# GpSimd takes the sums of h for both parts, and three weight loads are placed anew, in a two-layer trunk on one NeuronCore

## The chip, the cores and the metric

The kernel runs on one core of one Trainium2 chip, as one launch. The metric is the time of the whole launch in microseconds (us). Before the change, three runs gave 2854.96, 2854.89 and 2853.45 us; their median, 2854.89, is the time before. The profile comes from another execution, which took 2849.49 us. In the profile PE is the engine of the matmuls (PEld its weight loads), DVE the vector engine, ACT the scalar engine, POOL GpSimd, and SP the engine that issues the DMAs.

## The reference

One inference step of a trunk with two layers on 1024 frames of a new stream and 32 frames of a running one (1056 columns), width 1024. Layer 0 mixes with retention (4 heads), layer 1 with gated linear attention, GLA (4 heads); after each comes a convolutional feed-forward network of inner width 2816. Cut to what matters:

```
def conv_ffn(h, conv_state, w_up, conv_w, conv_b, w_down):
    u = h @ w_up
    ext = concatenate([conv_state, u], axis=1)
    c = conv_b + sum over j of ext[:, j:j + T] * conv_w[j]      # 3 taps
    gate, val = split(c, 2, axis=-1)
    return (silu(gate) * val) @ w_down, ext[:, T:]

def trunk(x, ...):
    for i in range(2):
        h = rmsnorm(x, norm_mix[i])
        y, S = retention_mixer(h, ...) if i == 0 else gla_mixer(h, ...)
        x = x + y
        h = rmsnorm(x, norm_ffn[i])
        y, cs = conv_ffn(h, ...)
        x = x + y
    return rmsnorm(x, norm_final), states and caches
```

## The kernel before

Every float32 operand of a matmul is split into a high and a low part, and a product takes three matmuls: high by high, high by low, low by high. ACT casts the high part (`whi`, `wgh`, `XA`), DVE subtracts it from the source for the low part (`wlo`, `wgl`). The large products work on pairs of weight tiles and pairs of column blocks with seven products in place of eight (`seven`, matmuls at L333, L337, L338; 264 columns each, 12 matmuls a product). For that, sums and differences of weights (`pair_weights`, L297 on, DVE at L310 to L316) and of activations are formed. `snap` copies a product from PSUM by ACT (L569, L1471, L1536); `put` adds one into its place by DVE (L1532).

The order of the instructions on every engine is made ahead: the program is written once, as a list of instructions with their dependencies, and a list scheduler with a cost model of its own then sets each engine's queue. `order(a, b)` puts a behind b. SP issues nearly all DMAs in its own order, and a DMA waits there for its buffer.

The stages, in us of the profile:

- 0 to 66, the opening: x comes in three column chunks `xc`, the first in four parts, and the first products of `w_rg` run (L124 to L126). `load_w` loads one 512 KB weight tile and splits it. Squares of x go to `NB` for the norm.
- 66 to 358, the pairs: gate, query and key projections, 14 pairs f. `operands(1)` prepares the second half of the columns in `NB` with eight scalings by ACT (L538) and sums by DVE (L543, L547), ahead of `load(0)`, the first pair's weights. The cosines and sines are multiplied by the norm R on DVE (L606).
- 358 to 905, retention and its output product.
- 909 to 1363, the up product of layer 0: `ffn_up` takes 22 f of 14 products, about 20.3 us each; after the last product of an f, `conv` convolves it and writes h to DRAM, `scr_h` (22 rows of tiles).
- 1363 to 1625, the down product: class `Pieces` takes h in two parts p of 8 tiles in the seven-product form, and the other 6 tiles follow plainly. Part one reads sums of h that are formed during the up product (`load_h`, `sum_h`, `sums_out`: four sums k of two tiles, DVE L1386, through `scr_s`); its operands come as 14 loads of 528 KB through a queue (`pull`, L1396). Part two loads 1.08 MB whole for each of four column blocks (`staged`, L1418) and forms its sums on DVE (`minus`, L1432, four for each s), just ahead of the casts (L1427).
- 1630 to 1960, GLA: four heads in three column chunks; the next head's weights `w_gqk` are loaded and split where they are first used (L104), the score tile A is masked (L1000, `copy_predicated`) and multiplied.
- 1960 to 2847, layer 1's output product, up product (2132 to 2590), down product and the last norm, with the same code.

Of the kernel before, what the change touches and what calls it, by code (L numbers as in the profile page):

```python
# [52 lines left out]
def trunk_kernel(ctx: ExitStack, tc: tile.TileContext, io):  # L53
# [45 lines left out]
    def load_w(src, dst=None, after=None):  # L99
        i = uid()  # L100
        raw = raw_tile(f"raw{i}")
        nc.sync.dma_start(raw, src)
        hi, lo = dst or (w_tile(f"whi{i}"), w_tile(f"wlo{i}"))
        ins = S.copy(hi, raw), V.tensor_tensor(lo, raw, hi.bitcast(F32), op=ALU.subtract)  # L104
        if after is not None:
            for a, b in zip(ins, after):
                order(a, b)
        return hi, lo

    ahead = {}  # L110
# [20 lines left out]
    sqb = [2]  # L131

    def sumsq(ss, kt, src, n, on_dve=False):
        def square(dst):
            if on_dve:
                V.tensor_tensor(dst, src, src, op=ALU.mult)
            else:
                S.activation(dst, src, AF.Square)
# [158 lines left out]
    def pair_weights(sa, sb):  # L297
# [5 lines left out]
        def split(src, name):  # L303
            h, l_ = w_tile(f"{name}h{uid()}"), w_tile(f"{name}l{uid()}")
            S.copy(h, src)  # L305
            V.tensor_tensor(l_, src, h.bitcast(F32), op=ALU.subtract)  # L306
# [3 lines left out]
        V.tensor_tensor(rv[:, a], rv[:, a], rv[:, b], op=ALU.add)  # L310
        V.tensor_tensor(rg[:, a], rv[:, a], rg[:, a], op=ALU.subtract)
        V.tensor_tensor(rg[:, b], rg[:, b], rg[:, a], op=ALU.subtract)
# [3 lines left out]
        V.tensor_tensor(rv[:, b], rv[:, b], rg[:, a], op=ALU.subtract)  # L316
# [89 lines left out]
    def opening(cs, SA, RE, NB, gn):  # L406
# [17 lines left out]
        xs, w01 = [], []  # L424
        sqb[0] = 4
        nps[0] = Arena(NB, ss=(384, 4), sq=(384, 4), dg=(384, 1), tm=(6, 2))
        with pool("x0", bufs=3, side="right") as xp:
            for c, (c0, n) in enumerate(CM):
                xc = xp.tile([P, KT, 384], F32, tag="xc", name=f"xc{c0}")
                step = 2 if c == 0 else 8  # L430
                for kt in range(0, KT, step):
                    nc.sync.dma_start(xc[:, kt:kt + step, :n], io["xT"][:, kt:kt + step, c0:c0 + n])
                    if c == 0 and kt in (0, 6):
                        w01.append(load_w(io["w_rg"][kt // 6]))
# [3 lines left out]
            nc.sync.dma_start(sin, io["sin"])  # L438
            nc.sync.dma_start(SA, io["xT"][:, :, 0:2 * TH])
# [67 lines left out]
    def pairs_phase(cs, SA, sp, UR, NB, gn, xp, finish, then):  # L507
# [19 lines left out]
        steps = []  # L527

        def operands(s):
# [7 lines left out]
            def scale(kt):  # L537
                return lambda: S.activation(st[:, kt], st[:, kt], AF.Copy, scale=gcol[:, 0, kt:kt + 1])  # L538
# [18 lines left out]
        X[1].update(zip((7, 4), rooms_of(sp.tile([P, 2 * sz], F32R, tag="SA", name="SA1"), 2)))  # L557
        operands(1)
        later(steps, 8)
# [7 lines left out]
        def snap(b):  # L567
            t = up.tile([P, TH], F32, tag="sn", name=f"sn{uid()}", bufs=6)
            S.copy(t, b)  # L569
# [1357 lines left out]
```

## Time and profile before

| what | value |
|---|---|
| median of three runs | 2854.89 us |
| the profiled execution's own time | 2849.49 us |
| its span | 2847.7 us |
| TensorE: first matmul starts at | 9.12 us |
| TensorE busy | 2784.6 us |
| DVE, ACT, POOL busy | 2109.5, 1320.2, 278.5 us |
| bytes moved by DMA | 419.35 MB, mean 147 GB/s |

The page's rows give an engine's busy time with its share of the span, and how many instructions it ran. A row of a timeline gives the start, the duration, the engine, the kernel's line, the operation and its tiles (out<-in), and in brackets how long the engine had stood idle ahead of it and what it waited for. In rows by line, "x24" is a count, and where three numbers stand behind it, they are the least, the median and the largest duration in ns.

### The profile page before, as it was taken

What the parts mean: (1) busy time and instruction counts of PE and PEld (TensorE: products, weight loads), DVE (VectorE), ACT (ScalarE), POOL (GpSimd) and SP (SyncE); (2) the same over time, 40 slices, a digit from 0 to 9 for tenths busy, and PEclk for the clock granted to TensorE, in tenths of its full rate; (3) what the DMA queues carried; (4) which work ended last, traced back from release to release, by engine and by line L of the source; (5) the groups of instructions that cost most, each with busy time, mean ns of one, the idle gap of its engine ahead of it and who ended that gap; (6) DMA issues with size and microseconds to landing.
All of it is one profiled execution on the core that took longest, in us unless ns stands there. A gap on an engine that the chain in (4) does not pass through costs nothing.

```text
span 2847.7 us, 52541 instructions
## 1 busy us (share of the span) xinstructions
PE 2784.6 (98%) x20954; PEld 2681.9 (94%) x20954; DVE 2109.5 (74%) x3506; ACT 1320.2 (46%) x2395; POOL 278.5 (10%) x516
## 2 busy tenths in 40 slices
PE   8999999999999999999999999999999999999998
PEld 7999977888999999999999899999999999999997
DVE  7777777777578877877775677774478878788756
ACT  8433344444455444445443555553245444445424
POOL 1000000000001111111000232220011111110001
PEclk9999999999999999999999999999999999999999
DMA  6333386664865223332866301114522233428673
GB/s 218 110 123 106 118 269 205 213 198 150 273 203 192 76 75 121 129 129 94 284 216 240 122 27 46 52 44 143 198 85 75 73 116 115 150 70 278 205 232 116
DMA packets 232326, 419.35 MB, mean 147 GB/s; under 512 B 27376, under 2 KB 145776, under 8 KB 231056
## 3 DMA queue, kind: packets, MB, share of 16 engines
q1 hardware_dynamic: 231536, 415.40, 43.6%
q8 instruction: 164, 2.69, 0.4%
q14 instruction: 82, 0.67, 0.1%
q10 hardware_dynamic: 544, 0.59, 0.1%
HBM read 292.08 MB, written 123.85 MB: 146 GB/s over the span
## 4 chain that ended last, share of the span: by engine, by line
PE 82%; DVE 7%; DMA 4%; ACT 4%; issue 1%; POOL 1%; SPq 0%; DVEq 0%; ACTq 0%; POOLq 0%
PE pu L338 16%; PE pu L333 16%; PE pu L337 16%; PE pd L1281 4%; PE pd L1280 4%; PE pd L1282 4%; PE psv L238 2%; PE psv L237 1%; PE psv L236 1%; PE pj L124 1%; PE pj L126 1%; PE pj L125 1%; PE pg L124 1%; PE pg L125 1%; PE pg L126 1%
## 5 line engine op out<-in xcount | busy, mean ns | idle before, releaser
L104 DVE TENSOR_TENSOR wlo<-raw,whi 128x1024 fp32r<-128x1024 f32 x146 | 180.7, 1241 | 100.9 <-ACT whi L104 44.9
L1536 ACT COPY AR<-pu 128x264 f32<-128x264 f32 x264 | 99.0, 375 | 295.2 <-PE pu L338 292.4
L338 PE MATMUL pu<-XA,wgl 128*128 128x264 f32 x752 | 213.6, 284 | 0.0
L333 PE MATMUL pu<-XA,wgh 128*128 128x264 f32 x752 | 213.0, 283 | 0.0
L337 PE MATMUL pu<-XA,wgh 128*128 128x264 f32 x752 | 213.0, 283 | 0.0
L104 ACT CAST whi<-raw 128x1024 fp32r<-128x1024 f32 x146 | 152.3, 1048 | 110.7 <-DMA raw<-w_ro 38.0
L1280 PE MATMUL pd<-XB,whi 128*128 128x264 f32 x552 | 157.9, 286 | 1.6 <-DVE rm L208 1.6
L1558 DVE SCALAR_TENSOR_TENSOR AR<-AR,cw 128x1058 f32<-128x1058 f32 x88 | 115.8, 1317 | 57.7 <-ACT AR L1557 57.4
L1282 PE MATMUL pd<-XB,wlo 128*128 128x264 f32 x552 | 157.0, 284 | 0.0
L1281 PE MATMUL pd<-XB,whi 128*128 128x264 f32 x552 | 156.7, 284 | 0.0
L333 PE MATMUL pu<-XA,wsh 128*128 128x264 f32 x520 | 148.6, 286 | 1.7 <-ACT AR L1536 0.9
L338 PE MATMUL pu<-XA,wsl 128*128 128x264 f32 x520 | 148.3, 285 | 0.8 <-DVE wsl L306 0.8
L337 PE MATMUL pu<-XA,wsh 128*128 128x264 f32 x520 | 147.7, 284 | 0.0
L1532 DVE TENSOR_TENSOR AR<-AR,pu 128x264 f32<-128x264 f32 (+2 forms) x440 | 144.6, 368 | 0.0
L306 DVE TENSOR_TENSOR wtl<-rv,wth 128x1024 fp32r<-128x1024 f32 x58 | 71.6, 1234 | 98.5 <-ACT wth L305 97.1
L333 PEld LDWEIGHTS pu<-XA,wgh 128*128 128x128 f32 x752 | 141.3, 188 | 0.0
L338 PEld LDWEIGHTS pu<-XA,wgl 128*128 128x128 f32 x752 | 141.2, 188 | 0.0
L337 PEld LDWEIGHTS pu<-XA,wgh 128*128 128x128 f32 x752 | 141.2, 188 | 0.0
L333 PE MATMUL pu<-XA,whi 128*128 128x264 f32 x448 | 127.5, 285 | 1.8 <-ACT XA L1427 1.2
L338 PE MATMUL pu<-XA,wlo 128*128 128x264 f32 x448 | 127.1, 285 | 1.6 <-DVE wlo L104 1.6
L337 PE MATMUL pu<-XA,whi 128*128 128x264 f32 x448 | 126.9, 284 | 0.5 <-DVE XA L1412 0.3
L333 PE MATMUL pu<-XA,wth 128*128 128x264 f32 x408 | 116.4, 285 | 0.7 <-ACT wth L305 0.7
(481 smaller groups left out, 10528.0 us busy)
## 6 DMA issues: line engine op xcount, KB each, us to landing
raw<-w_ro SPq DMA_DIRECT2D x52, 512.0 KB, 4.7
rg<-w_up SPq DMA_DIRECT2D x44, 512.0 KB, 3.6
rv<-w_up SPq DMA_DIRECT2D x44, 512.0 KB, 3.5
scr_h<-AR SPq DMA_DIRECT2D x44, 512.0 KB, 2.7
AR<-scr_x SPq DMA_DIRECT2D x32, 528.0 KB, 4.9
scr_x<-AR SPq DMA_DIRECT2D x32, 528.0 KB, 3.5
raw<-scr_w SPq DMA_DIRECT2D x32, 512.0 KB, 4.8
AR<-scr_h SPq DMA_DIRECT2D x28, 528.0 KB, 4.8
```

The source lines that it names most:

```text
L104: ins = S.copy(hi, raw), V.tensor_tensor(lo, raw, hi.bitcast(F32), op=ALU.subtract)
L124: PE.matmul(ps, hi[:, k], rh, start=kt == 0, stop=False)
L306: V.tensor_tensor(l_, src, h.bitcast(F32), op=ALU.subtract)
L333: mm = PE.matmul(ps, wh[:, k], x[:, 0, kt], start=m in (1, 2, 4, 5) and kt == 0, stop=False, skip_group_check=True)
L337: PE.matmul(ps, wh[:, k], x[:, 1, kt], start=False, stop=False, skip_group_check=True)
L338: mm = PE.matmul(ps, wl[:, k], x[:, 0, kt], start=False, stop=kt == 3, skip_group_check=True)
L1280: PE.matmul(o, w[0][:, k], h[0][:, :n], start=i == 0, stop=False)
L1281: PE.matmul(o, w[0][:, k], h[1][:, :n], start=False, stop=False)
L1282: self.last_mm = PE.matmul(o, w[1][:, k], h[0][:, :n], start=False, stop=i == nk - 1)
L1532: V.tensor_tensor(u[:, d:d + n], t[:, o:o + n], b[:, o:o + n], op=op)
L1536: S.copy(t, b)
L1558: V.scalar_tensor_tensor(cj, uj[:, 1:T + 3], cw[:, nt, 1:2], cj, op0=ALU.mult, op1=ALU.add)
```

## The change

Five parts.

1. Opening. `load_w` may load, cast and subtract in halves; the first weight tile does so, with a part of x between. The small load `rgn` goes behind `sin`. The squares of the first chunk come behind the cast of the second weight tile.
2. Start of the pairs. `load(0)` is written ahead of `operands(1)`, whose scalings come behind the last cast of the weights or the last snapshot; cosine and sine are multiplied by GpSimd. `pair_weights` takes the engine of its sums: GpSimd for f = 1 and 2 of the pairs and f = 1 of each up product.
3. Sums of h for both parts: eight of four instructions each in a layer (before: four), on GpSimd, at the products `SUMS`; `scr_s` grows from 4 to 8.
4. Part two of the down product reads its operands through the same queue as part one (28 loads of 528 KB through four slots); `staged` and the sixteen subtractions are gone.
5. GLA. The next head's `w_gqk` are loaded in chunk 1 of a head, and the low parts are ordered behind that chunk's last mask.

```diff
-    def load_w(src, dst=None, after=None):
+    def load_w(src, dst=None, parts=1, between=None):
...
+        for j in range(parts):
+            k = slice(j * D // parts, (j + 1) * D // parts)
+            nc.sync.dma_start(raw[:, k], src[:, k])
+            last_w[:] = S.copy(hi[:, k], raw[:, k]), V.tensor_tensor(lo[:, k], raw[:, k], hi[:, k].bitcast(F32),
+                                                                     op=ALU.subtract)
+            if between and j + 1 < parts:
+                between()
...
-    def pair_weights(sa, sb):
+    def pair_weights(sa, sb, E=V):
...
-        V.tensor_tensor(rv[:, a], rv[:, a], rv[:, b], op=ALU.add)
+        E.tensor_tensor(rv[:, a], rv[:, a], rv[:, b], op=ALU.add)
...
+                if c == 0:
+                    part(0, 2)
+                    w01.append(load_w(io["w_rg"][0], parts=2, between=lambda: part(2, 2)))
+                    part(4, 2)
+                    part(6, 2)
+                    w01.append(load_w(io["w_rg"][1]))
+                    first_w[:] = last_w
+                else:
+                    part(0, KT)
...
             nc.sync.dma_start(sin, io["sin"])
+            nc.sync.dma_start(gn, io["rgn"])
...
-                    sumsq(stage[c], kt, xs[c][:, kt, :CM[c][1]], CM[c][1])
+                    sumsq(stage[c], kt, xs[c][:, kt, :CM[c][1]], CM[c][1], first_w[0] if c == 0 else None)
...
+                    ins = S.activation(st[:, kt], st[:, kt], AF.Copy, scale=gcol[:, 0, kt:kt + 1])
+                    if s:
+                        order(ins, snaps[-1] if snaps else last_w[0])
...
-            W[f] = pair_weights(*src)
+            W[f] = pair_weights(*src, G if f in (1, 2) else V)
...
         load(0)
+        X[1].update(zip((7, 4), rooms_of(sp.tile([P, 2 * sz], F32R, tag="SA", name="SA1"), 2)))
+        operands(1)
+        later(steps, 2)
...
-                V.tensor_tensor(t, t, R, op=ALU.mult)
+                G.tensor_tensor(t, t, R, op=ALU.mult)
...
-            later(steps, 1)
+            later(steps, 3 if n in (0, 2) else 1)
...
+            h, c = u
+            if c == 1 and h + 1 < GH:
+                for j in range(2):
+                    preload(("w_gqk", h + 1, j))
+                    order(last_w[1], mask[0])
...
+    SUMS = (42, 56, 70, 84, 97, 109, 121, 133)
...
-                order(nc.sync.dma_start(self.v[:, a], scr_h[k + 4 * a].rearrange("p (q t) -> p q t", q=4)), after)
+                order(nc.sync.dma_start(self.v[:, a], scr_h[k + k // 4 * 4 + 4 * a].rearrange("p (q t) -> p q t", q=4)),
+                      after)
...
-            V.tensor_tensor(d, a, b, op=ALU.subtract)
+            G.tensor_tensor(d, a, b, op=ALU.subtract)
...
-    def part_one(self):
-            for s in range(2):
+    def operands(self):
+            for p, s in ((0, 0), (0, 1), (1, 0), (1, 1)):
...
-            self.todo += [split(1, b11), minus(b12, b12, b11), split(2, b21), split(5, b12), minus(b12, b22, b12),
-                          split(6, b12), minus(b11, b12, b11), split(7, b11), minus(b21, b12, b21), split(4, b21),
-                          split(3, b22)]
...
-                        if s:
-                            for j in range(2):
-                                self.staged(1, s, j)
-                        self.operands(s)
+                        self.splits()
...
-                    self.step()
+                    self.step(1 if p or q else 2)
...
-            W[f] = pair_weights(io["w_up"][l, f], io["w_up"][l, NF + f])
+            W[f] = pair_weights(io["w_up"][l, f], io["w_up"][l, NF + f], G if f == 1 else V)
...
-            if s == 1 and i % 2 == 0 and 8 <= f <= 16 and f % 2:
-                nxt.sum_h(i // 2)
-            if s == 0 and i == 5 and 8 <= f <= 16:
-                if f % 2 == 0:
-                    if f > 8:
-                        nxt.sums_out((f - 10) // 2)
-                    if f < 16:
-                        nxt.load_h((f - 8) // 2, stored[0])
+            for j, at in enumerate(SUMS if s == 0 else ()):
+                if k == at + 12:
+                    nxt.sums_out(j)
+                if k == at:
+                    nxt.load_h(j, stored[0])
+                if k - at in (5, 7, 9, 11):
+                    nxt.sum_h((k - at - 5) // 2)
```

Three places show what the scheduler makes of it. The first is ACT's queue at the start of the pairs, from the first pair's first cast (`wg`) to the first snapshot (`sn`, the copy of the first product); RE is the gate that the opening leaves, NB the second half of the columns, being scaled. Before:

```order
L305 CAST wgh_649<-rg_645 128x1024
L379 ACTIVATE RE_84<-RE_84 128x768
L383 ACTIVATE RE_84<-RE_84,rgn 128x384 x2
L538 ACTIVATE NB_628<-NB_628,gcol 128x528 x8
L379 ACTIVATE RE_84<-RE_84 128x576
L314 CAST wv_656<-rv_646 128x512
L383 ACTIVATE RE_84<-RE_84,rgn 128x288 x2
L305 CAST wsh_660<-rg_645 128x1024
L569 COPY sn_681<-pu_668 128x264
```

And with the change:

```order
L309 CAST wgh_641<-rg_637 128x1024
L382 ACTIVATE RE_83<-RE_83 128x768
L317 CAST wv_648<-rv_638 128x512
L386 ACTIVATE RE_83<-RE_83,rgn 128x384 x2
L309 CAST wsh_652<-rg_637 128x1024
L309 CAST wth_656<-rv_638 128x1024
L382 ACTIVATE RE_83<-RE_83 128x576
L551 ACTIVATE NB_661<-NB_661,gcol 128x528
L386 ACTIVATE RE_83<-RE_83,rgn 128x288 x2
L551 ACTIVATE NB_661<-NB_661,gcol 128x528
L582 COPY sn_678<-pu_665 128x264
L551 ACTIVATE NB_661<-NB_661,gcol 128x528 x4
```

Six of the eight scalings now stand behind the first snapshot (one and one ahead of it, four right behind), and the cast of `wt` has come ahead of it.

The second is SP's queue in the down product, around the first weight loads of the part's last pairs; L1480, L1489 and their successors L1482, L1491 bring the residual and store a result. Before, with the two whole loads of part two's first half (L1418):

```order
L1480 DMA AR_7512<-scr_x 128x2x528
L102 DMA raw_15949<-w_dn 128x1024
L1489 DMA scr_x<-AR_7512 256x1x528
L1480 DMA AR_7512<-scr_x 128x2x528
L102 DMA raw_15955<-scr_w 128x1024
L102 DMA raw_15961<-scr_w 128x1024
L1418 DMA AR_7512<-scr_h 128x8x264
L1489 DMA scr_x<-AR_7512 256x1x528
L1418 DMA AR_7512<-scr_h 128x8x264
L1444 DMA rv_15968<-w_dn 128x512
```

With the change, where the pieces come by L1420 (the first of the three from `scr_h` ends part one, the next two begin part two):

```order
L1491 DMA scr_x<-AR_7515 256x1x528
L1482 DMA AR_7515<-scr_x 128x2x528
L1420 DMA AR_7515<-scr_h 128x4x264 x3
L1420 DMA AR_7515<-scr_s 128x4x264
L1491 DMA scr_x<-AR_7515 256x1x528
L1482 DMA AR_7515<-scr_x 128x2x528
L1420 DMA AR_7515<-scr_s 128x4x264 x2
L105 DMA raw_15983<-w_dn 128x1024
L1491 DMA scr_x<-AR_7515 256x1x528
L105 DMA raw_15989<-scr_w 128x1024
L105 DMA raw_15995<-scr_w 128x1024
```

The five pieces that open part two now stand ahead of the weight load that the two whole loads stood behind.

The third is the place of the sums of h in the up product: before on DVE, between the puts (L1532), convolutions (L1558, L1562) and weight splits (L306):

```order
L1562 TENSOR_TENSOR AR_7512<-AR_7512 128x1058
L310 TENSOR_TENSOR rv_11959<-rv_11959 128x512
L306 TENSOR_TENSOR wtl_11746<-rv_11727,wth_11745 128x1024
L1532 TENSOR_TENSOR AR_7512<-AR_7512,pu_11886 128x232
L1532 TENSOR_TENSOR AR_7512<-AR_7512,pu_11886 128x32
L1532 TENSOR_TENSOR AR_7512<-AR_7512,pu_11931 128x264
L1532 TENSOR_TENSOR AR_7512<-AR_7512,pu_11831 128x264
L1386 TENSOR_TENSOR AR_7512<-AR_7512 128x2x264 x2
L1558 SCALAR_TENSOR_TENSOR AR_7512<-AR_7512,cw_7506 128x1058
L306 TENSOR_TENSOR wgl_11963<-rg_11958,wgh_11962 128x1024
```

and with the change on POOL, where all four stand together between the copies of one convolution into the cache (L1549, L1550):

```order
L1541 COPY AR_7515<-cc_7510 128x2
L1549 COPY cst_7511<-AR_7515 128x2
L1550 COPY cst_7511<-AR_7515 128x2
L1410 TENSOR_TENSOR AR_7515<-AR_7515 128x2x264 x4
L1549 COPY cst_7511<-AR_7515 128x2
L1550 COPY cst_7511<-AR_7515 128x2
L1541 COPY AR_7515<-cc_7510 128x2
```

The four sums of a group have left DVE's queue and follow one another on POOL with nothing between them.

More of the change, by code (lines that the diff above doesn't have):

```diff
@@ L97, in w_tile @@
         return wp.tile([P, D], F32R, tag="w", name=name, bufs=10)
-    def load_w(src, dst=None, after=None):
+    def load_w(src, dst=None, parts=1, between=None):
         i = uid()
         raw = raw_tile(f"raw{i}")
-        nc.sync.dma_start(raw, src)
         hi, lo = dst or (w_tile(f"whi{i}"), w_tile(f"wlo{i}"))
[L104 to L107, printed above, removed]
+        for j in range(parts):
[5 more added lines that the diff above has]
+                between()
         return hi, lo
+    last_w = []
     ahead = {}
@@ L131, in trunk_kernel, with sumsq @@
     sqb = [2]
-    def sumsq(ss, kt, src, n, on_dve=False):
+    last_sq = [None]
+    def sumsq(ss, kt, src, n, after=None):
         def square(dst):
[L135 to L138, printed above, removed]
+            ins = S.activation(dst, src, AF.Square)
+            if after is not None:
+                order(ins, after)
+            last_sq[0] = ins
         s_ = ss[kt % len(ss)]
@@ L1025, in gla @@
         state = {}
+        mask = [None]
         def mix(h, c, u):
```

58 lines of the change are left out of this document (16 added, 42 removed).

## Prediction

> **What bounds the kernel now.** I read the busy shares first, then the chain that ended last, then windows cut along the stages. In the window rows, "TensorE busy" is the second number, the share near the end is the granted clock, and the difference between window length and PE busy is time TensorE stood still.
>
> ```profile
> PE 2784.6 (98%) x20954; PEld 2681.9 (94%) x20954; DVE 2109.5 (74%) x3506; ACT 1320.2 (46%) x2395; POOL 278.5 (10%) x516
> PE 82%; DVE 7%; DMA 4%; ACT 4%; issue 1%; POOL 1%; SPq 0%; DVEq 0%; ACTq 0%; POOLq 0%
> core 0: us, PE busy (x) PEld busy (x) DVE busy (x) ACT busy (x) POOL busy (x), PEclk, DMA share, GB/s
> 0.00:66.00 66.00, 55.62 (x332) 54.03 (x333) 49.26 (x76) 53.18 (x96) 12.06 (x17) 1.00 0.68 234
> 66.00:77.00 11.00, 7.45 (x48) 7.03 (x47) 10.47 (x12) 10.94 (x17) 0.00 (x0) 0.84 0.24 86
> 905.00:940.00 35.00, 32.44 (x255) 31.31 (x255) 32.04 (x52) 17.05 (x29) 2.49 (x5) 1.00 0.26 77
> 940.00:1340.00 400.00, 400.00 (x3299) 400.00 (x3298) 320.82 (x471) 183.12 (x258) 55.53 (x139) 1.00 0.30 104
> 1092.40:1112.70 20.30, 20.30 (x170) 20.30 (x169) 16.88 (x26) 9.13 (x14) 3.13 (x7) 1.00 0.38 132
> 1340.00:1385.00 45.00, 42.17 (x335) 40.76 (x334) 41.39 (x49) 32.40 (x40) 3.37 (x8) 1.00 0.81 259
> 1450.00:1470.00 20.00, 17.81 (x126) 16.84 (x125) 14.09 (x17) 7.52 (x10) 0.00 (x0) 0.91 0.75 257
> 1630.00:1960.00 330.00, 322.96 (x2701) 305.54 (x2699) 244.33 (x595) 179.82 (x578) 87.61 (x125) 0.99 0.14 45
> 2675.00:2695.00 20.00, 17.29 (x133) 16.25 (x132) 14.55 (x17) 8.09 (x12) 0.00 (x0) 1.00 0.81 273
> ```
>
> TensorE is busy for 98% of the span, and the change removes none of its matmuls. So all that can be won lies in TensorE's holes and in the slow clock behind them. The rows size the holes: 10.4 us in 0 to 66, 3.55 us in 66 to 77, 2.6 at the start of the up product, none at all between 940 and 1340, 2.8 around the change to the down product, 2.2 and 2.7 in the two 20 us windows at the down product's second part, 7.0 over GLA's 330 us. Work taken from another engine inside 940 to 1340 gains nothing, however large it is; there the only question is whether a hole appears.
>
> **The change part by part.** *Opening.*
>
> ```profile
> 1.19 0.42 SPq L67 DMA_DIRECT2D rgn<-rgn  x1
> 1.66 4.44 DMA xc<-xT
> 6.19 1.12 ACT L153 ACTIVATE XA<-xc,gcol 128x384 fp32r<-128x384 f32 x2 [4.18 <-DMA xc<-xT]
> 7.22 0.92 ACT L138 ACTIVATE NB<-xc 128x384 f32<-128x384 f32 x2
> 8.04 1.03 ACT L104 CAST whi<-raw 128x1024 fp32r<-128x1024 f32 x1
> 9.12 0.69 PE L124 MATMUL pj<-XA,whi 128*128 128x384 f32 x1 [9.12 <-ACT whi L104]
> 17.27 0.44 PE L126 MATMUL pj<-XA,wlo 128*128 128x384 f32 x1 [0.59 <-DVE wlo L104]
> ```
>
> SP issues the small rgn load at 1.19 and the first x at 1.66; with rgn moved behind sin, x goes 0.47 us earlier and ACT's split of x ends near 6.84 instead of 7.31. Behind it stood two squares (0.92 us) and a whole cast (1.03 us). Now the squares wait for a later cast, and the cast of half a weight comes next, about 0.52 us: TensorE starts near 7.4 in place of 9.12, which is 1.7 us, and the stop of 0.59 us at 17.27 goes, since the low half is also ready in halves. That is 2.3 us at most; I count 1.9, because x's later parts still come at the loads' pace and one more transfer is now interleaved.
>
> *Start of the pairs.*
>
> ```profile
> 55.55 1.25 DVE L606 TENSOR_TENSOR cos<-cos,R 128x1056 f32<-128x1056 f32 x1
> 62.94 5.13 ACT L538 ACTIVATE NB<-NB,gcol 128x528 f32<-128x528 f32 x8 [0.35 <-DMA NB<-xT]
> 69.92 1.04 ACT L305 CAST wsh<-rg 128x1024 fp32r<-128x1024 f32 x1
> 71.28 0.39 PE L333 MATMUL pu<-XS,wsh 128*128 128x264 f32 x1 [2.41 <-ACT sn L569]
> 72.93 0.59 PE L338 MATMUL pu<-XS,wsl 128*128 128x264 f32 x1 [1.14 <-DVE wsl L306]
> ```
>
> The two stops, 2.41 and 1.14 us, make up the whole 3.55 us of the window, and its clock of 0.84 over 11 us costs another 0.16 x 11 = 1.8 us: 5.3 in all. Both come from ACT and DVE being full (10.94 and 10.47 of 11). ACT's eight scalings (5.13 us) now stand mostly behind the first snapshot: six of eight leave, 3.85 us, and one cast (1.04) comes ahead, so the snapshot can run 2.8 us earlier; that covers the 2.41. I leave 0.9 us of holes, so 4.4. Against it stand the cosine and sine products on GpSimd, which this stage has not shown; the price is worked out next: 2.9 us each, where DVE took 1.25. At worst DVE is held for their whole length, 2 x (2.9 - 1.25) = 3.3 us; nearest to a partial hold I take 1.3. Opening and pairs' start together: 1.9 + 4.4 - 1.3 = **5.0 gained**, between 2 and 8 (the 2.3 and 5.3, and a little of what TensorE loses between).
>
> *Sums of h.* DVE's sums leave, GpSimd's come, twice as many: 8 groups of 4 per layer, 64 of 528 elements.
>
> ```profile
> L1386 DVE TENSOR_TENSOR AR<-AR x32: 700/703/709, 1099.5 to 2465.4; 128x528 f32<-128x528 f32 x32
> L149 POOL TENSOR_TENSOR ss<-ss,sq x39: 747/987/1792, 766.6 to 2816.5; 128x264 f32<-128x264 f32 x24, 128x384 f32<-128x384 f32 x12, 128x288 f32<-128x288 f32 x3
> L198 POOL TENSOR_TENSOR ss<-ss,ss 128x384 f32<-128x384 f32 x2 | 2.1, 1070 | 0.2
> L1786 POOL TENSOR_TENSOR AR<-AR,R 128x576 f32<-128x576 f32 x1 | 1.9, 1914 | 6.4 <-DVE R L217 6.4
> 1657.40 0.34 DVE L951 TENSOR_TENSOR x<-d,q 128x192 f32<-128x192 f32 x1
> 1659.87 0.83 POOL L943 TENSOR_TENSOR d<-b 128x384 f32<-128x384 f32 x1 [0.96 <-DVE x L951]
> 1659.92 0.99 DVE L951 TENSOR_TENSOR x<-d,q 128x192 f32<-128x192 f32 x1
> 1097.27 1.23 DVE L306 TENSOR_TENSOR wtl<-rv,wth 128x1024 fp32r<-128x1024 f32 x1 [2.62 <-ACT wth L305]
> 1102.12 0.29 PE L338 MATMUL pu<-XA,wtl 128*128 128x264 f32 x1
> ```
>
> The shortest 264 element addition on GpSimd is 747 ns and one of 384 is 1070: 2.7 ns an element, so 1.46 us for 528, 1.42 for 512, 2.9 for 1056 (estimates). The dearest neighbour is 1.91 for 576. GpSimd has the room: 3.1 us busy of 20.3 per f. The danger is DVE. The last rows show the same DVE instruction at 0.34 us alone and at 0.99 when GpSimd had started 0.05 us before it and ran 0.83: it sat nearly until GpSimd ended. So four sums in a row can hold DVE for 4 x 1.46 = 5.8 us, less where DVE is idle or takes an input from PSUM (the puts); DVE is busy 16.88 of 20.30 and some of that is puts, so I take two thirds, 3.9. DVE has two cushions before TensorE notices: it stood 2.62 us idle for the cast ahead of wtl, and wtl, written at 1098.50, was first read at 1102.12, 3.62 later. Together 6.24 against 3.9: no hole. I charge 0.5 for a few bad alignments, between 0 and 22 (below); relief of DVE is worth nothing here.
>
> The Trainium skill, "SBUF — State Buffer", "Who interferes with whom", speaks against this move: a DVE instruction with two SBUF inputs contends with a GpSimd instruction that reads SBUF, and the later one is blocked for the other's whole length. The pair at 1659.9 agrees with it. By the rule without any idle share the hold is the 5.8 us above, still under the cushions by 0.4 us.
>
> *Start of the up product.* f = 1's pair sums move to GpSimd in both layers: four instructions of 1.42 replace four near 0.7 (by the 528 element row). DVE, 32.04 of 35 busy in 905 to 940, gets 2.8 us, and the sums take 5.7 instead of 2.8 in their own chain. The 2.56 us of holes there can close, or 2.9 us can be added: I take **1.0 gained** for both layers, between -3 and +4. The same edit for two f of the pairs stage has cover: 77 to 340 holds no hole.
>
> *Down product, second part.*
>
> ```profile
> 1450.17 7.98 DMA AR<-scr_h
> 1458.17 1.07 ACT L1427 CAST XA<-AR 128x1056 fp32r<-128x1056 f32 x1 [2.64 <-DMA AR<-scr_h]
> 1467.05 0.39 PE L333 MATMUL pu<-XB,whi 128*128 128x264 f32 x1 [0.55 <-ACT XB L1427]
> 2692.05 0.39 PE L333 MATMUL pu<-XB,whi 128*128 128x264 f32 x1 [1.88 <-ACT XB L1427]
> 1452.00:1458.00 6.00, 5.96 (x50) 1.00 0.99 334
> ```
>
> Two 1.08 MB loads land 7.98 us after issue, at 1458.15, ACT waits 2.64 for them, and TensorE stands behind it. Now 528 KB pieces come through four slots, issued far ahead, and no subtraction lies between load and cast; 16 subtractions leave DVE. Window arithmetic gives what is to be had: 2.19 + 0.09 x 20 = 4.0 in layer 0 and 2.7 in layer 1, so 6.7. But the last row (PE busy, clock, DMA share, GB/s) shows the DMA engines at 0.99 just then, and the new scheme moves 28 x 528 KB a layer in place of 14 and four large ones. I count **6.0**, between 1 and 9. Around 1340 to 1385 (2.8 us of holes, DMA share 0.81) more pulls stand ahead of weight loads in SP's order; I take 0, between -2 and +1.
>
> *GLA.*
>
> ```profile
> 1668.84 1.23 DVE L104 TENSOR_TENSOR wlo<-raw,whi 128x1024 fp32r<-128x1024 f32 x1 [2.00 <-ACT whi L104]
> 1673.33 0.88 PE L995 MATMUL pl<-x 128*128 128x64 f32 x6 [0.85 <-DVE A L989]
> ```
>
> DVE splits the next head's weights ahead of the score product A, and TensorE waits 0.85 us. With the splits behind the masks that stop goes: **0.9 gained**, 0 to 1.5; late next are Al and kl, which now stand behind the same two splits (2 x 1.23) but are read only after the score products.
>
> *Sum:* 5.0 - 0.5 + 1.0 + 6.0 + 0.9 = 12.4 us. Against the profiled execution, 2849.49 us (span 2847.7), that is 2837.1. The median of the runs shown, 2854.89, lies 5.4 above it, so I forecast 2842.5, rounded to **2842**.
>
> **Rivals.** (a) *GpSimd holds DVE too long*, slower. Place: the f of the up product with sums. The point from which it decides is a hold of 6.24 us per group, 1.56 a sum. At the 576 element row's 1.91 the hold is 7.6, so TensorE loses 1.4 us in each of 16 groups, 22 us: 2842 + 22 = 2864. For it: DVE is 83% busy there and the pair at 1659.9. Against: it needs every sum at the dearest price with no idle time hit. The cited rule is this mechanism.
> (b) *The second part stays bound by loads*: 0.99 DMA share says the pieces queue instead of the whole. Then 1 of 6 us comes: 2842 + 5 = 2847. Against: SP's new order issues the first pieces several loads ahead of where the old ones stood, so they have longer to land.
> (c) *The holes reappear*: (b), and ACT and DVE, still full at 66, give back 3 us of the opening's 5: 2842 + 5 + 3 = 2850, no measurable change.
> (d) *All terms at their upper ends*: 8 + 4 + 9 + 1.5 + 1 = 23.5, half of the surplus over 12.4 is 5.6: 2836, down to 2831.
>
> **How the numbers follow.** Forecast 0.53, (b) 0.16, (c) 0.13, (a) 0.10, (d) 0.08. A measurement of this kernel tells some 0.2% from no change, 5.7 us: faster is below 2849.2, slower above 2860.6. Faster is forecast, (b) and (d): 0.77; the same is (c): 0.13; slower is (a): 0.10. The likeliest case alone spans 2836 to 2847; (b) and (c), each known to about 5 us (the unknown at the up product's start), carry the range to 2857, and 2832 takes in most of (d). Left out are (a) and a bit of (d).
>
> **What would show it.** First matmul near 7.4 in place of 9.12; no stop above 1 us between 63 and 75; no hole in 940 to 1340 (holes there that follow DVE's wtl or wsl are rival (a), and DVE instructions of doubled length beside GpSimd's sums its sign); the casts at L1435 not waiting for a load near 1450 (waiting is (b)); no 0.85 us stop before GLA's first head. The forecast is wrong if a GpSimd sum takes over 1.56 us alone, or if the pulls push a weight load past its cast.

## The result, and the profile after

The changed kernel takes 2870.8 us in the median of four runs (2864.99 to 2873.78), the kernel before 2854.17 beside it: a ratio of 1.0058, with an interval of 1.0042 to 1.0073. It is slower by some 0.6%, where 2842 was forecast. The profiled execution took 2864.99 us, with a span of 2863.1, 15.4 us more than before's.

The first lines of the profile's page, the first matmul in the timeline, and windows of the same stages as before's (window; then busy time and instructions of TensorE, its weight loads, DVE, ACT and POOL; clock, DMA share, GB/s):

```profile
PE 2782.5 (97%) x20954; PEld 2677.3 (94%) x20954; DVE 2122.6 (74%) x3441; ACT 1318.9 (46%) x2396; POOL 436.9 (15%) x598
PE 74%; DVE 13%; DMA 5%; ACT 4%; issue 3%; POOL 1%; SPq 0%; DVEq 0%; ACTq 0%; POOLq 0%
6.86 0.69 PE L127 MATMUL pj<-XA,whi 128*128 128x384 f32 x1 [6.86 <-ACT whi L106]
66.00:77.00 11.00, 7.07 (x39) 6.10 (x39) 6.76 (x7) 10.27 (x17) 1.28 (x1) 0.84 0.41 124
77.00:100.00 23.00, 20.12 (x160) 19.41 (x159) 16.80 (x18) 11.35 (x16) 7.35 (x4) 1.00 0.18 59
940.00:1340.00 400.00, 393.88 (x3227) 392.00 (x3226) 329.19 (x447) 179.40 (x253) 108.80 (x168) 1.00 0.35 124
1030.00:1340.00 310.00, 303.88 (x2488) 302.21 (x2487) 256.43 (x340) 135.21 (x192) 94.87 (x135) 1.00 0.39 137
1450.00:1470.00 20.00, 18.27 (x149) 17.84 (x148) 17.62 (x21) 11.28 (x15) 0.00 (x0) 1.00 0.92 314
```

Two things stand out against before. DVE runs 65 instructions fewer and is busy 13 us longer; and the up product, where TensorE stood not at all between 940 and 1340, has 6.1 us of holes there. In the chain of work that ended last, DVE's share went from 7% to 13%.

To see where the 15 us come from, each matmul's start was set beside the start of the same matmul of before. The table gives, for the changed kernel and for eight of the experiments below, how much each stage adds to (+) or takes from (-) that difference, in us. The first two letters name the run.

| stage (us of before) | changed | e1 | e2 | e3 | e4 | e5 | e8 | e9 | e10 |
|---|---|---|---|---|---|---|---|---|---|
| opening, to 49 | -1.9 | -1.3 | -0.6 | -2.0 | -1.7 | -1.5 | -1.1 | -1.1 | -1.3 |
| pairs, 49 to 340 | +4.4 | +4.5 | -0.9 | +4.6 | +4.1 | -0.8 | +1.1 | -0.6 | +4.4 |
| retention and up product's start, to 930 | -0.7 | -0.7 | -1.9 | +1.0 | +4.3 | -0.4 | -3.0 | -1.9 | +4.7 |
| up product, layer 0, to 1353 | +8.3 | 0.0 | +11.6 | +1.3 | +10.4 | 0.0 | 0.0 | 0.0 | -0.1 |
| down product, layer 0, to 1600 | -1.3 | -2.3 | -2.2 | -2.6 | -3.8 | -2.0 | -3.7 | -2.6 | -2.5 |
| GLA, to 1950 | -2.4 | -2.1 | -2.3 | -2.3 | -1.4 | -2.4 | -2.3 | -2.4 | -2.3 |
| to the up product, layer 1, 2200 | +0.9 | +0.1 | -0.4 | +0.8 | +2.3 | -1.2 | -1.2 | -1.2 | +0.9 |
| up product, layer 1, to 2560 | +8.6 | 0.0 | +7.9 | 0.0 | +9.6 | 0.0 | 0.0 | 0.0 | 0.0 |
| down product, layer 1, to 2830 | -0.6 | +0.8 | +0.5 | +2.8 | +0.2 | -1.1 | +0.7 | +1.9 | -1.3 |

The third row holds no edit but the last few us of it, and goes from -3 to +5. Two kernels were profiled twice: e5 and e11, one kernel, had -0.4 and +2.3 there, e9 and e12, another, -1.9 and +3.5, and their spans differ by 6.1 and 10.0 us. So a span alone can't tell 10 us here, and the rows of the edited stages are what the experiments are read by. Between two profiles of one kernel the opening, the pairs and the up products agree within 0.2 us, the other rows differ by up to 5.4. Where the border at 49 is drawn moves up to 0.7 us between the first two rows of every column; their sum stays.

How a hole in the up product comes about stands in the timelines (start, duration, engine, line, operation). POOL and DVE of the changed kernel (POOL's four sums first as one row, then the last three of them one by one), then TensorE, and last the window behind the hole (us, TensorE's busy time, clock, DMA share, GB/s):

```profile
1082.93 7.77 POOL L1410 TENSOR_TENSOR AR<-AR 128x528 f32<-128x528 f32 x4 [1.07 <-DMA AR<-scr_h]
1084.34 2.35 POOL L1410 TENSOR_TENSOR AR<-AR 128x528 f32<-128x528 f32 x1
1086.77 2.20 POOL L1410 TENSOR_TENSOR AR<-AR 128x528 f32<-128x528 f32 x1
1088.92 1.78 POOL L1410 TENSOR_TENSOR AR<-AR 128x528 f32<-128x528 f32 x1
1084.19 1.32 DVE L1552 SCALAR_TENSOR_TENSOR AR<-AR,cw 128x1058 f32<-128x1058 f32 x1 [1.89 <-ACT AR L1551]
1085.43 2.35 DVE L309 TENSOR_TENSOR wgl<-rg,wgh 128x1024 fp32r<-128x1024 f32 x1
1087.69 1.82 DVE L318 TENSOR_TENSOR wv<-rv,wv 128x512 fp32r<-128x512 f32 x1
1089.43 1.81 DVE L314 TENSOR_TENSOR rg<-rv,rg 128x512 f32<-128x512 f32 x1
1091.17 0.38 DVE L1526 TENSOR_TENSOR AR<-AR,pu 128x232 f32<-128x232 f32 x1
1094.01 0.42 DVE L1526 TENSOR_TENSOR AR<-AR,pu 128x264 f32<-128x264 f32 x1
1094.48 0.39 PE L336 MATMUL pu<-XA,wsh 128*128 128x264 f32 x1 [1.01 <-DVE AR L1526]
1094.60:1097.00 2.40, 2.40 (x20) 1.00 0.04 10
```

And the same instructions before:

```profile
1082.34 1.22 DVE L306 TENSOR_TENSOR wgl<-rg,wgh 128x1024 fp32r<-128x1024 f32 x1
1083.47 0.69 DVE L315 TENSOR_TENSOR wv<-rv,wv 128x512 fp32r<-128x512 f32 x1
1084.08 0.69 DVE L311 TENSOR_TENSOR rg<-rv,rg 128x512 f32<-128x512 f32 x1
1087.52 0.42 DVE L1532 TENSOR_TENSOR AR<-AR,pu 128x264 f32<-128x264 f32 x1
1090.23 0.28 PE L333 MATMUL pu<-XA,wsh 128*128 128x264 f32 x1
```

While POOL's four sums run, three DVE instructions take 1.13, 1.13 and 1.12 us longer: a hold of 3.4 us. Everything in DVE's queue behind them moves by that, the put at 1087.52 too, which empties the PSUM bank that the next product of `wsh` writes. Before, it ended at 1087.94 and TensorE came at 1090.23: 2.3 us to spare. 3.4 - 2.3 = 1.1, and the hole is 1.01.

From the first sum's end on, the two engines end in turn: DVE at 1085.51, POOL at 1086.69, DVE at 1087.78, POOL at 1088.97, DVE at 1089.51, POOL at 1090.70, DVE at 1091.24. `wv`, 0.69 us alone, started at 1087.69 and ended 0.54 us behind the sum's end at 1088.97. Had the two engines shared the time evenly, it would have taken at most twice 0.69, 1.38 us (an estimate); it took 1.82. So here one waits for the other's end.

The other groups follow the same sum. For the eight groups of layer 0, by their start, the table gives how much longer DVE's instructions took than the median of the same instructions in e5, where GpSimd has no sums, and the hole of TensorE behind them, in us:

| group at | 1040 | 1083 | 1124 | 1165 | 1207 | 1249 | 1273 | 1313 |
|---|---|---|---|---|---|---|---|---|
| DVE held | 3.39 | 3.38 | 2.45 | 2.96 | 3.39 | 2.59 | 4.21 | 2.77 |
| hole | 1.01 | 1.01 | 0.07 | 0.58 | 1.01 | 0.21 | 1.84 | 0.39 |

The hole is the hold less 2.38 us each time, within 0.01, and it is so in layer 1's eight groups too (holds of 2.64 to 4.44). The holes add up to 6.1 us, while the table of stages has 8.3: behind a hole the first matmul takes 0.39 us where the others take 0.28, and the next ones start later, some 0.3 us a hole.

### The profile page after: what moved, and what is told of

It reads as the page before. It is cut to its first block, busy times and chain, and to the rows that moved or that the text cites. A ratio compares the mean times of both kernels' runs of the same rounds, so it can differ in the third digit from the quotient of the medians.

```text
span 2863.1 us, 52689 instructions
## 1 busy us (share of the span) xinstructions
PE 2782.5 (97%) x20954; PEld 2677.3 (94%) x20954; DVE 2122.6 (74%) x3441; ACT 1318.9 (46%) x2396; POOL 436.9 (15%) x598
## 4 chain that ended last, share of the span: by engine, by line
PE 74%; DVE 13%; DMA 5%; ACT 4%; issue 3%; POOL 1%; SPq 0%; DVEq 0%; ACTq 0%; POOLq 0%
PE pu L336 14%; PE pu L341 13%; PE pu L340 13%; PE pd L1303 3%; PE pd L1304 3%; PE pd L1302 3%; PE psv L242 2%; PE psv L241 2%; PE psv L240 2%; DVE wgl L309 2%; PE pj L127 1%; PE pj L128 1%; PE pj L129 1%; DVE wv L318 1%; PE pg L127 1%
## 5 line engine op out<-in xcount | busy, mean ns | idle before, releaser
L106 DVE TENSOR_TENSOR wlo<-raw,whi 128x1024 fp32r<-128x1024 f32 (+1 forms) x147 | 179.8, 1229 | 96.5 <-PE pu L340 44.7
L106 ACT CAST whi<-raw 128x1024 fp32r<-128x1024 f32 (+1 forms) x147 | 152.6, 1042 | 108.5 <-DMA raw<-w_ro 39.4
L153 POOL TENSOR_TENSOR ss<-ss,sq 128x264 f32<-128x264 f32 (+2 forms) x39 | 38.5, 987 | 705.9 <-ACT sq L139 703.1
L1551 ACT ACTIVATE AR<-AR,cw 128x1058 f32<-128x1058 f32 x88 | 111.9, 1271 | 56.2 <-DVE AR L1526 52.7
L336 PE MATMUL pu<-XA,whi 128*128 128x264 f32 x448 | 127.3, 284 | 2.1 <-ACT AR L1473 2.1
```

The lines of the kernel that those rows point to most:

```text
L106: last_w[:] = S.copy(hi[:, k], raw[:, k]), V.tensor_tensor(lo[:, k], raw[:, k], hi[:, k].bitcast(F32), op=ALU.subtract)
L336: mm = PE.matmul(ps, wh[:, k], x[:, 0, kt], start=m in (1, 2, 4, 5) and kt == 0, stop=False, skip_group_check=True)
L1551: S.activation(cj, uj[:, 2:T + 4], AF.Identity, scale=cw[:, nt, 2:3], bias=cw[:, nt, 3:4])
```

## The experiments

Each kernel is the changed one with the edit shown, unless it says otherwise; each was compared with the kernel before on the same chip.

**e1: the sums of h on DVE.**

```diff
-            G.tensor_tensor(d, a, b, op=ALU.subtract)
+            V.tensor_tensor(d, a, b, op=ALU.subtract)
```

> The changed kernel with one edit: the sums of h are done by the vector engine again (64 instructions of 0.70 us), still for both parts, with the same loads and stores. Theory (GpSimd's four sums in a row hold the vector engine 3.4 us, and the put that gives back a PSUM bank has only 2.45 us to spare): the eight holes in each up product go, the two up products lose nothing against the kernel before instead of 8.3 and 8.6 us, span 2863.1 - 17 = about 2846. Rival (twice the loads and stores of h, or the vector engine's order itself, makes the holes): the holes stay at the same places and the span stays within 3 us of 2863.

Measured: 2852.0 us, ratio 1.0004 (0.9994 to 1.0013), span 2846.8. Both up products lose nothing, with the same doubled loads and stores and with DVE doing twice the sums of before:

```profile
1030.00:1340.00 310.00, 310.00 (x2557) 310.00 (x2556) 259.72 (x384) 140.03 (x198) 44.56 (x107) 1.00 0.40 139
```

That is the window that had 303.88 us of TensorE in the changed kernel. DVE's busy time is 3.3 us more than there and does no harm. The rival falls: the loss hangs on GpSimd.

**e3: the same sums on GpSimd, spaced out.** The order puts each sum behind the matmuls of the product at which it is written, so that they stand between the copies of the convolution.

```diff
-        def sum_h(self, j):
+        def sum_h(self, j, mm):
...
-            G.tensor_tensor(d, a, b, op=ALU.subtract)
+            order(G.tensor_tensor(d, a, b, op=ALU.subtract), mm)
...
-                    nxt.sum_h((k - at - 5) // 2)
+                    nxt.sum_h((k - at - 5) // 2, mm)
```

> The changed kernel with each of the four sums of a group, still on GpSimd, placed in the order behind the matmuls of the product at which it is written, so that they no longer run in a row but lie between the copies that wait for the vector engine. Theory (the hold must add up past the 2.45 us of the put): a single sum holds the vector engine 1.1 us, no holes or holes under 0.3 us in the up products, span 2846 to 2849. Rival (GpSimd's total of 6 to 8 us a group counts, or its sums are late for their store): holes of the same sum, span near 2863.

Measured: 2854.55 us, ratio 1.0016 (1.0007 to 1.0026), span 2851.3; 1.3 us lost in layer 0's up product, at its last group. In layer 1 the last group has a hole of 0.75 us too, at 2579.99; it falls in the table's last row. The sums by line (least, median and largest ns), changed and spaced, and the spaced kernel's window:

```profile
L1410 POOL TENSOR_TENSOR AR<-AR x64: 1321/1787/2352, 1039.8 to 2549.7; 128x528 f32<-128x528 f32 x64
L1410 POOL TENSOR_TENSOR AR<-AR x64: 1322/1332/3625, 1050.7 to 2557.2; 128x528 f32<-128x528 f32 x64
1030.00:1340.00 310.00, 310.00 (x2557) 310.00 (x2556) 256.66 (x350) 139.91 (x198) 95.44 (x139) 1.00 0.37 134
```

A sum takes 1.32 us alone; in a row beside DVE the median is 1.79, since each also waits for DVE. Spaced out, the same work on the same engine makes no hole between 1030 and 1340. The waiting as such has hardly gone: the mean of a sum is 1.78 us (changed: 1.84), and over layer 0's up product DVE's instructions still take 18.7 us longer than in e5 (changed: 25.2). It only no longer falls into one stretch. The span is 2 us above the range expected; the table puts that in its third row and its last.

**e10: half of each sum, four in a row.** This asks how the loss grows with the hold; the other half of the columns is left out.

```diff
-            G.tensor_tensor(d, a, b, op=ALU.subtract)
+            h = TH // 2
+            G.tensor_tensor(d[:, :, :h], a[:, :, :h], b[:, :, :h], op=ALU.subtract)
```

> The changed kernel with the sums of h on GpSimd, four in a row as changed, but over half of each sum's columns (the other half is left out). Theory (a put has 2.45 us to spare, and only what the hold takes beyond that shows): each sum near 1 us, the hold some 1.7 us a group, so no holes in the up products or holes of a few tenths, span 2846 to 2849. Rival (holes in proportion to GpSimd's busy time): half of the 17 us stays, span near 2855.

Measured: span 2850.3, and the two up products lose nothing, with 64 sums of 1.20 us still in a row:

```profile
L1411 POOL TENSOR_TENSOR AR<-AR x64: 746/1198/1849, 1045.7 to 2537.2; 128x264 f32<-128x264 f32 x64
1030.00:1340.00 310.00, 310.00 (x2557) 310.00 (x2556) 250.37 (x354) 140.62 (x199) 78.70 (x139) 1.00 0.39 138
```

Two thirds of GpSimd's time and none of the loss: it isn't in proportion, there is a threshold, as a spare time of a put makes one. DVE is held 0.6 to 1.7 us a group here, less than 2.38 in all sixteen. The span again missed its range from above, by 1.3 us, outside these stages (+4.4 at the pairs, +4.7 in the stage without edits).

**e2: cosine, sine and the pair sums on DVE.**

```diff
-            W[f] = pair_weights(*src, G if f in (1, 2) else V)
+            W[f] = pair_weights(*src)
...
-                G.tensor_tensor(t, t, R, op=ALU.mult)
+                V.tensor_tensor(t, t, R, op=ALU.mult)
...
-            W[f] = pair_weights(io["w_up"][l, f], io["w_up"][l, NF + f], G if f == 1 else V)
+            W[f] = pair_weights(io["w_up"][l, f], io["w_up"][l, NF + f])
```

> The changed kernel with cosine, sine and the pair sums of f = 1 and 2 (and f = 1 of each up product) on the vector engine again. If GpSimd's hold makes the stops at the start of the pairs (the vector engine's sums at L563 took 2.35 and 2.10 us there in place of 1.25): some 2 of the 5.1 us lost between 59 and 112 us come back, span about 2861. If the new order of loads and stores makes them: less than 0.7 us comes back.

Measured: 2863.67 us, ratio 1.0041 (1.0026 to 1.0056), span 2859.5. The pairs go from +4.4 to -0.9: 5.3 us, more than twice what was expected, so GpSimd's hold is the larger part of the loss there. In the changed kernel's timeline GpSimd's pair sums and DVE's sums of columns lie on one another:

```profile
71.81 1.28 POOL L313 TENSOR_TENSOR rv<-rv 128x512 f32<-128x512 f32 x1 [13.41 <-DMA rv<-w_rg]
79.06 2.18 POOL L315 TENSOR_TENSOR rg<-rg 128x512 f32<-128x512 f32 x1
81.20 2.30 POOL L319 TENSOR_TENSOR rv<-rv,rg 128x512 f32<-128x512 f32 x1
72.11 2.10 DVE L563 TENSOR_TENSOR NB<-NB 128x1056 f32<-128x1056 f32 x1 [2.79 <-issue]
75.65 0.43 DVE L630 TENSOR_TENSOR RE<-sn,pu 128x264 f32<-128x264 f32 x1 [1.44 <-DMA scr_g<-RE]
77.74 2.35 DVE L563 TENSOR_TENSOR NB<-NB 128x1056 f32<-128x1056 f32 x1
80.69 3.92 DVE L559 TENSOR_TENSOR XA<-NB,XA 128x1056 fp32r<-128x1056 f32 x2
```

The sums at L563 take 2.10 and 2.35 us where they take 1.25 alone, and two at L559 3.92, alone 2.42. Cosine and sine (3.01 and 2.98 us on GpSimd, from 52.44 to 58.39) hold DVE as well: its product at L474 takes 3.05 us beside them and 0.75 in e2, two sums at L559 4.69 and 2.42, in all 4.6 us. e2 takes both kinds back at once, so how the 5.3 divides between them isn't shown. A part of it is clock: 0.84 in the changed kernel's window 66 to 77, 1.00 in e2's.

The up products, where e2 keeps the changed sums, lose 11.6 us in layer 0 instead of 8.3. Their holes have nearly the same sizes (6.6 us in all); what is added is clock. The windows 932 to 936 and 1279.8 to 1284 show 0.57 and 0.59, and e4's windows 1289 to 1293 and 2521 to 2525 show 0.57.

**e4 and e8: the old order at the start of the pairs**, with GpSimd's moves (e4) and without any of them (e8). Both edits are the same:

```diff
-                    if s:
-                        order(ins, snaps[-1] if snaps else last_w[0])
...
+        X[1].update(zip((7, 4), rooms_of(sp.tile([P, 2 * sz], F32R, tag="SA", name="SA1"), 2)))
+        operands(1)
+        later(steps, 8)
         UA = Arena(UR(), u=(4 * TH, 3), rv=(4 * TH, 1))
...
         load(0)
-        X[1].update(zip((7, 4), rooms_of(sp.tile([P, 2 * sz], F32R, tag="SA", name="SA1"), 2)))
-        operands(1)
-        later(steps, 2)
...
-            later(steps, 3 if n in (0, 2) else 1)
+            later(steps, 1)
```

> The changed kernel with the order at the start of the pairs put back: the operands of the second half ahead of the first pair's weights, no scaling held behind a snapshot, one step after each product; GpSimd still does cosine, sine and the pair sums. If the new order makes the five new stops between 66 and 97 us: about 5 us come back (the old two stops of 2.4 and 1.1 us with the start 2.3 us earlier), span about 2858. If GpSimd makes them: under 2 us.

> The kernel without GpSimd's moves, with the order at the start of the pairs put back as before the change. If the new order is worth what was forecast (4.4 us): the time rises by 4 us, with the old stops of 2.4 and 1.1 us. If the old stops were only moved: within 1.5 us of the same time.

Measured: e4 2870.4 us, ratio 1.0056 (1.0037 to 1.0075), span 2871.7; the pairs give +4.1 instead of +4.4, so with GpSimd in the way the order is worth nothing. e8 2847.95 us, ratio 0.9993 (0.9981 to 1.0006), span 2838.3; the pairs give +1.1, against -0.8 with the new order (e5): the order is worth 1.9 us there once GpSimd is gone. Most of that is clock: 0.84 in e8's window 66 to 77, as before, and 1.00 in e5's. By this stage both guesses for e8 missed, and the truth lay between; by the medians on one chip e8 is 4.6 us slower than e5, but its runs spread from 2840.1 to 2855.4 and the two spans are within 0.1 us.

**e5 and e11: none of the moves to GpSimd** (the edits of e1 and e2 together), run twice.

> The changed kernel without any of its moves to GpSimd: sums of h, pair sums, cosine and sine all on the vector engine; opening, order at the pairs, part two's queue and GLA as changed. If GpSimd's holds are the whole loss: the 17 us of the up products and the 4 us at the start of the pairs come back, span 2863.1 - 21 = 2842, some 0.2% under the kernel before. If something else of the change costs time too: span 2846 or more.

> The kernel without GpSimd's moves once more, beside the one with the old part two on the same chip. If the new queue is worth the 6 us forecast, it is 6 us faster than its neighbour; if its stops were only moved, 2 to 3 us or less.

Measured: 2843.32 us, ratio 0.9973 (0.9962 to 0.9984), span 2838.4; the second time 2846.13 us, ratio 0.9986 (0.9977 to 0.9995), span 2844.5. This kernel is faster than the changed one and the one before, the latter by 0.1 to 0.3%. What is left of the change gains 4 to 7 us in the medians, where the whole lost 17. Its pairs, in the windows that carried the stops:

```profile
66.00:77.00 11.00, 8.61 (x67) 8.08 (x66) 8.35 (x11) 10.47 (x18) 0.00 (x0) 1.00 0.37 122
77.00:100.00 23.00, 21.78 (x172) 20.89 (x172) 15.71 (x20) 10.46 (x16) 0.00 (x0) 1.00 0.26 82
70.44 0.69 DVE L313 TENSOR_TENSOR rv<-rv 128x512 f32<-128x512 f32 x1 [2.41 <-DMA rv<-w_rg]
72.21 0.42 DVE L630 TENSOR_TENSOR RE<-sn,pu 128x264 f32<-128x264 f32 x1
72.69 0.39 PE L336 MATMUL pu<-XS,wv 128*128 128x264 f32 x1 [1.64 <-DVE RE L630]
```

TensorE is busy 30.4 of 34 us here, 27.2 in the changed kernel, and the clock stays at 1.00. The largest stop left, 1.64 us, waits for the put at 72.21. That put shows no wait of its own; it stands in DVE's queue behind the first pair sum of f = 1 (L313), for whose weights DVE stood idle 2.41 us. In the changed kernel, where GpSimd forms that sum, the same put waits for the store of the gate, `scr_g<-RE` (its row at 75.65 above). SP's timelines of the changed kernel, the store in its chain of work, SP's timeline of before, and the put there show that store's place:

```profile
68.21 0.34 SPq L304 DMA_DIRECT2D rv<-w_rg  x1
69.35 0.35 SPq L303 DMA_DIRECT2D rg<-w_rqk  x1
69.90 0.38 SPq L387 DMA_DIRECT2D scr_g<-RE  x1
69.90 5.46 DMA scr_g<-RE
...
70.05 0.36 SPq L384 DMA_DIRECT2D scr_g<-RE  x1
72.90 0.35 SPq L300 DMA_DIRECT2D rv<-w_rg  x1
72.79 0.42 DVE L614 TENSOR_TENSOR RE<-sn,pu 128x264 f32<-128x264 f32 x1
```

The store goes out at the same time as before, but now behind two 512 KB loads, and lands 5.46 us later; before, the put shows no wait for it.

**e9 and e12: the old part two of the down product**, with no move to GpSimd either: the kernel before with the new opening, the new order at the pairs and GLA's weights behind the masks. The code of `Pieces` and the sums of h are the old ones, whole; run twice, the second time beside e11.

> The kernel before with the new opening, the new order at the start of the pairs and GLA's weights behind the masks; nothing on GpSimd that was not there, and the down product with four large loads and subtractions as before, four sums of h a layer. If part two's queue is worth the 6 us forecast: 6 us slower than the kernel without GpSimd's moves, span near 2844.5. If its stops were only moved (2.0 and 1.1 us gained by that kernel's trace): 2 to 4 us slower, span near 2841.5.

> The kernel without GpSimd's moves and with the old part two once more: 0.2% faster than the kernel before by opening, order at the pairs and GLA alone, and 2 to 3 us slower than its neighbour if the queue's stops were only moved, 6 if the forecast of the queue holds.

Measured: 2846.06 us, ratio 0.9979 (0.9968 to 0.9990), span 2839.6; then 2846.40 us, ratio 0.9985 (0.9976 to 0.9994), span 2849.6, beside e11's 2846.13. Side by side the queue is worth 0.3 us, which can't be told from nothing. In the table e9, without the queue, has -2.6 and +1.9 at the two down products, e5, with it, -2.0 and -1.1.

**e7: without the residual's traffic** around part two (its loads and stores in the last pair of part one and the first of part two are left out), on top of e5.

```diff
-                    nc.sync.dma_start(C[u][1], home(u))
+                    if (p, q) not in ((0, 3), (1, 0)):
+                        nc.sync.dma_start(C[u][1], home(u))
...
-                    nc.sync.dma_start(home(u), c)
+                    if (p, q) not in ((0, 3), (1, 0)):
+                        nc.sync.dma_start(home(u), c)
```

> The kernel without GpSimd's moves, that leaves out the loads and stores of the residual in the last pair of part one and the first pair of part two of the down product (some 4.3 MB a layer less in about 40 us). Theory (the second part is bound by loads, since 14 pieces of 528 KB a half bring 3.2 MB more than the old four large loads): the stops of about 5 us between 1410 and 1475 shrink to under 2 in each layer, 4 to 8 us less in all. Rival (the order of the scalar engine, not the rate of the loads): under 2 us less.

Measured: 2841.48 us, ratio 0.9967 (0.9955 to 0.9980), span 2839.7. That is 1.8 us less than e5 in the medians, on the same chip. The down products take 2.8 and 2.2 us less than before's, e5's 2.0 and 1.1: 1.9 us for 4.3 MB a layer (against e11, whose layer 1 came out 2.3 us longer than e5's, 4.0). The theory asked for 4 to 8. So the rate of the loads is at most a part of what binds there. What stays is in the timelines of e7's ACT and TensorE:

```profile
1444.01 1.08 ACT L1435 CAST XA<-AR 128x1056 fp32r<-128x1056 f32 x1 [1.14 <-DMA AR<-scr_h]
1445.61 1.07 ACT L1435 CAST XA<-AR 128x1056 fp32r<-128x1056 f32 x1 [0.52 <-DMA AR<-scr_h]
1446.59 0.37 ACT L1473 COPY AR<-pu 128x264 f32<-128x264 f32 x1
1447.01 0.39 PE L336 MATMUL pu<-XB,whi 128*128 128x264 f32 x1 [1.57 <-ACT AR L1473]
```

The casts wait for pieces of h, the snapshot stands behind them, and TensorE waits 1.57 us for the snapshot.

**e6: casts behind snapshots**, on top of e5: each cast of part one and two is ordered behind the last snapshot written before it.

```diff
+            self.snapped = None
...
-                S.copy(self.X[s][m][:, 0], v)
+                ins = S.copy(self.X[s][m][:, 0], v)
+                if self.snapped:
+                    order(ins, self.snapped)
...
-                S.copy(t, b)
+                self.snapped = S.copy(t, b)
```

> The kernel without GpSimd's moves, with each cast of the scalar engine for the down product ordered behind the last snapshot written before it. Theory (TensorE's stops near 1417 and 1448 are snapshots that stand behind a cast that waits for its load): 2 to 4 us less than without this edit. Rival (the operand itself is late, not the snapshot): the stop moves to the operand, within 1 us of the same time or longer.

Measured: 2851.51 us, ratio 0.9999 (0.9989 to 1.0008), span 2850.4. The down products go from -2.0 and -1.1 in e5 (-2.2 and +1.2 in e11) to +0.1 and +2.8: 4 to 6 us worse, and 8.2 in the medians beside e5. The stop is now at the operand, as the rival had it:

```profile
1463.29 0.39 PE L336 MATMUL pu<-XA,whi 128*128 128x264 f32 x1 [1.70 <-ACT XA L1436]
```

## Why the prediction was wrong

*Opening: right.* The first matmul starts at 6.86 in place of 9.12, 2.3 us earlier, and 1.9 of it is left at 49, as counted (0.6 to 2.0 in the eight experiments of the table, all with this opening).

*Sums of h: the step that failed.* The hold was near: 3.9 us a group forecast, 2.5 to 4.4 measured, 3.2 in the mean, and a sum alone takes 1.32 us, under the 1.46 estimated. What failed is the sentence "DVE has two cushions before TensorE notices": the 6.24 us were those of one consumer, the weight piece wtl. The queue behind the held instructions held others, and the shortest spare time decides: a put with 2.38 us. So rival (a)'s mechanism came true, but with a wrong point of decision: a hold of 2.38 us, not of 6.24. The hold already forecast, 3.9, was beyond the true point. That its price lies near (22 forecast, 16.9 measured: 8.3 and 8.6 in the two layers) is luck: it took the surplus of a hold of 7.6 over 6.24, both too large. Runs e1, e3 and e10 show it from three sides: no GpSimd, no row, half the length, and between 1030 and 1340 each time no hole; the table of the eight groups shows it within the changed kernel. The Trainium skill's rule cited in the prediction ("SBUF — State Buffer", "Who interferes with whom") has the later engine blocked for the other's whole length, and the ends in turn at 1085 to 1091 agree with it.

*Start of the pairs: a gain forecast, a loss measured.* 4.4 was counted for the new order and 1.3 for GpSimd's hold by cosine and sine. The order is worth 1.9 (e5 against e8): the stop for the snapshot shrank, and a put came late instead, behind the next weights: in the changed kernel its store stands behind them in SP's new order, in e5 a pair sum that needs them stands ahead of it in DVE's queue. GpSimd costs 5.3 (changed against e2, or e1 against e5), four times what was counted, and over the 3.3 given as the worst. Cosine and sine had been counted, and hold DVE 4.6 us, while 2.5 us of its work left it (two products of 1.25): 2.1 in the balance, against the 1.3 taken. The pair sums of f = 1 and 2 were taken as covered, because 77 to 340 showed no hole, and that failed. A stage in which TensorE has no holes can still have little to spare: DVE was busy 16.80 us of 23 there with the change, its held time included, and the puts came late.

*Part two: mis-sized.* 6.0 was forecast; the changed kernel's trace shows 1.3 and 0.6, no more than e9 gains in layer 0 without the queue (2.6), and the runs side by side show 0.3. The old stop at the casts did go. In its place came snapshots behind casts in ACT's queue, which wait for pieces, as rival (b) had it in outcome; of its reason, that the loads' rate binds, e7 leaves at most a part. What was overlooked is that a piece can only be issued when a cast has emptied one of four slots, so that it comes no earlier than that allows; that this alone sets the stops is argued, not shown.

*GLA: right, and too small.* 0.9 forecast, 2.4 measured in the changed kernel, 1.2 to 2.4 in the other runs; the stop of 0.85 us ahead of the first head is gone. In the changed kernel clock comes on top: 1.00 in the window 1630 to 1960, where before had 0.99. What the rest is isn't shown.

*Start of the up product:* 1.0 forecast; with the pair sums of f = 1 on GpSimd the approach to layer 1's up product adds 0.1 to 2.3 us in the five kernels of the table that have them there; without them it takes 0.4 to 1.2 off, and nothing in e12. No run shows the gain; the sign points the other way, by little more than the 1.2 us by which e9 and e12, one kernel, differ there. In layer 0 the stage's own scatter hides it.

## What to carry to other kernels

When an engine is held or delayed, don't take the spare time of the one consumer in view: list what stands behind the held instruction in its queue, and take the shortest spare time among all who wait for those. Work moved to GpSimd beside a full DVE costs by its longest unbroken row: the same 64 sums lost 17 us in rows of four and about 2 spaced out, though DVE still waited three quarters as long in all. And a stage in which TensorE never stands still can have any amount of spare time, from plenty to none; only the distance from each result to its first use tells.

## What had not been expected of the hardware

The hold goes both ways: GpSimd's sum of 528 elements takes 1.32 us alone and 1.79 in the median when DVE works beside it, up to 2.35. Single holes don't settle the granted clock: behind the changed kernel's holes of 1.01 and 1.84 us in the up product the windows show 1.00, behind e2's hole of 1.84 us 0.59, and behind two stops of 1.01 and 1.00 us that end at 67.86 and 69.37 the changed kernel's window 70 to 74 shows 0.57. And retention, with no edit in it, differs by up to 5.4 us between two profiles of one kernel.
